# One transfer for the first weights of two pairs, sums inside the first pass, and no accumulating transfers, in a hybrid decoder step

## The chip, the cores and the metric

The kernel runs on one core of one Trainium2 chip. The metric is the device time of one execution in microseconds (us), lower is better. TensorE (PE) multiplies; VectorE (DVE), ScalarE (ACT) and GpSimd (POOL) work on elements; SyncE (SP) issues most transfers between the chip's memory and the core's on-chip memory.

## The reference: what is computed

One layer of a decoder for 256 new prompt tokens and 8 sequences of 4 new tokens each, 288 tokens in all, in float32. D_MODEL is 2048, the two head groups are 1024 wide each, the MLP is 8192 wide.

```python
def trunk_layer(x, hist_conv, hist_pool, pos0, ...):
    h = rmsnorm(x, norm1_g)
    proj = jnp.einsum("btd,de->bte", h, w_in) + b_in
    a, gate, z = proj[..., :D_CONV], proj[..., D_CONV:2 * D_CONV], proj[..., 2 * D_CONV:]
    u = a * jax.nn.sigmoid(gate)
    u_ext = jnp.concatenate([hist_conv, u], axis=1)
    c = jax.nn.silu(layernorm(depthwise_causal_conv(u_ext, conv_w, conv_b), ln_g, ln_b))
    z_ext = jnp.concatenate([hist_pool, z], axis=1)
    d = multiscale_pool(z_ext, pos0)          # window means (2, 4, 8, 16) minus z
    p = jnp.einsum("btgc,gce->btge", d, pool_w).reshape(bsz, T, D_POOL) * pool_scale
    x = x + jnp.einsum("btm,md->btd", jnp.concatenate([c, p], axis=-1), w_out)
    h2 = rmsnorm(x, norm2_g)
    f = jnp.square(jax.nn.relu(jnp.einsum("btd,df->btf", h2, w_ff1)))
    x = x + jnp.einsum("btf,fd->btd", f, w_ff2)
    return x, u_ext[:, -(CONV_W - 1):], z_ext[:, -(POOL_MAX - 1):]
```

A last RMSNorm follows, and the last 30 columns of u and 15 of z are returned too. The convolution has 31 taps.

## The kernel before, in words

Channels lie on the 128 partitions, the 288 tokens along the free side. Every product is made of float32 numbers split in two: `whi` is the weight rounded by a cast on ScalarE (L245), `wlo` the rest. A product of one 128x128 block takes three matmuls: `whi` by the high part of the activation (L284), `whi` by its low part (L285), `wlo` by the high part (L286). `gemm` runs over 16 blocks `k` of the contraction and two output halves `m`, 96 matmuls of 288 columns in all.

Weights arrive as tiles `wr` of 128x1024 (four k, both m) from a pool of six buffers, and their two parts lie in pools of five buffers each. `split_part` makes the low part in one of three ways, which the table `WAYS` picks by stage and turn: V subtracts on VectorE (L250), G on GpSimd in two halves (L253), D lets ScalarE write minus the high part into `wlo` (L247) and then has GpSimd issue a transfer that reads the weights once more from memory and adds them to it (L248). In the stage of the input projection D is taken once in each of the five blocks c3 to c7 and once in each of the four blocks p0 to p3.

The order of the work: a first pass makes the projections c0 and c1 ("both pairs") while x and the first weights land, k by k, in pieces (`first_pieces`, `first_split`). The norm's scale is not known by then; the pass multiplies x times the norm's gain, and `squares` sums the squares of x on ScalarE and VectorE. `rsqrt_sums` sums these over the channels with one-column matmuls on TensorE (`pt`, L211) and takes the inverse root; `spread` brings it to all partitions with a matmul (L230), and ScalarE copies it to `rb`. Then come the blocks of `SEQUENCE`: c2 to c7 (a convolution channel block each, with `conv_pair` behind it), p3 to p0 (the pooling groups) and P3 to P0 (their small products). `conv_pair` makes 31 products and sums on VectorE into `pc` and lastly into `c` (L398), with low priority, and GpSimd adds up `sum_c` (L407).

Then the output projection: its pooling half for the 8 column groups (`project_pool`, three groups before the layer norm of c and five in the middle of it), with the layer norm between: the mean on TensorE (`pmean`, L496), squares, `rsqrt_sums`, `spread`, then `n` on VectorE (L510), SiLU on ScalarE (L513), the high part by a cast (L515) and the low part on VectorE (L516) into `mx`, which the convolution half of the projection multiplies. The MLP runs in four chunks of 2048 columns.

Each engine runs its instructions strictly in the order in which they stand. A scheduler sets that order when the program is built, from priorities and its own timing of a simulated execution; the chip's timing has no part in it.

## Time and profile before

| | us |
|---|---|
| runs of the kernel | 1120.42, 1119.5, 1112.89 (median 1119.5) |
| the profiled execution | 1119.96 |
| its span, first to last instruction | 1118.2 |
| TensorE busy in the span | 1095.2 (98%) |
| VectorE, ScalarE, GpSimd busy | 628.6, 480.1, 178.4 |
| mean granted TensorE clock | 0.988 |

The profile names an instruction by its line in the kernel, its engine, its operation and its tiles (written tile, arrow, read tiles). Busy time of matmuls that overlap is counted once. "<-" behind an idle time names what the engine waited for. The granted clock is 1.00 at full speed. Times in windows are us from the start of the span.

### The profile page before, as it was taken

How to read it: one execution, taken by the hardware profiler on the slowest of the kernel's cores; microseconds unless marked ns; L12 is line 12 of the kernel's file. 1: busy time of each engine (PE TensorE's matmuls, PEld its weight loads, DVE VectorE, ACT ScalarE, POOL GpSimd, SP SyncE). 2: the span in 40 equal slices, each digit the busy share in tenths (PEclk: the TensorE clock that was granted, in tenths of full speed). 3: DMA queues.
4: the chain of work that ended last, by engine and by line, in shares of the span. 5: the costliest groups of instructions: out<-in, count | busy, mean ns of one | idle time of the engine just before them, and what ended most of it. 6: DMA issues, size and time to landing. Idle time of an engine off the chain costs nothing.

```text
span 1118.2 us, 19782 instructions
## 1 busy us (share of the span) xinstructions
PE 1095.2 (98%) x8214; PEld 1091.9 (98%) x8214; DVE 628.6 (56%) x825; ACT 480.1 (43%) x595; POOL 178.4 (16%) x217
## 2 busy tenths in 40 slices
PE   8999979999999999999999999999999999999995
PEld 8999979999999999999999999999999999999994
DVE  7599997668654544445554444544544445554453
ACT  8544544466444433334443333444433334444441
POOL 0689977903100000000000000000000000000000
PEclk9999999999999999999999999999999999999997
DMA  9886667545454455545555455554455544555522
GB/s 309 260 231 182 195 177 191 189 152 178 162 164 163 165 169 169 165 165 164 168 170 163 167 164 168 170 165 163 164 169 169 164 164 165 169 170 163 167 68 85
DMA packets 58553, 191.76 MB, mean 171 GB/s; under 512 B 6368, under 2 KB 11488, under 8 KB 58464
## 3 DMA queue, kind: packets, MB, share of 16 engines
q1 hardware_dynamic: 56880, 185.65, 50.6%
q0 software_dynamic: 1296, 4.72, 2.4%
q8 instruction: 64, 1.05, 0.4%
q14 instruction: 25, 0.20, 0.0%
q10 hardware_dynamic: 288, 0.14, 0.0%
HBM read 186.20 MB, written 4.28 MB: 170 GB/s over the span
## 4 chain that ended last, share of the span: by engine, by line
PE 93%; DMA 3%; POOL 1%; DVE 1%; ACT 0%; SPq 0%; issue 0%; DVEq 0%; POOLq 0%; ACTq 0%
PE ac L284 31%; PE ac L286 31%; PE ac L285 30%; DMA wlo<-in_w 3%; DMA wr<-in_w 1%; PE pt L211 1%; POOL wlo L253 1%; DVE xT L600 0%; POOL prd L402 0%; ACT whi L245 0%; PE pt L230 0%; POOL s L427 0%; PE pp L284 0%; SPq L176 0%; SPq L173 0%
## 5 line engine op out<-in xcount | busy, mean ns | idle before, releaser
L245 ACT CAST whi<-wr 128x1024 fp32r<-128x1024 f32 (+2 forms) x350 | 356.4, 1021 | 580.0 <-PE ac L285 558.4
L250 DVE TENSOR_TENSOR wlo<-wr,whi 128x1024 fp32r<-128x1024 f32 (+2 forms) x300 | 358.9, 1199 | 354.7 <-ACT whi L245 353.8
L284 PE MATMUL ac<-ax,whi 128*128 128x288 f32 x1024 | 303.2, 296 | 0.0
L284 PE MATMUL ac<-fx,whi 128*128 128x288 f32 x1024 | 303.1, 296 | 0.0
L286 PE MATMUL ac<-fx,wlo 128*128 128x288 f32 x1024 | 301.9, 295 | 0.0
L286 PE MATMUL ac<-ax,wlo 128*128 128x288 f32 x1024 | 301.8, 295 | 0.0
L285 PE MATMUL ac<-ax,whi 128*128 128x288 f32 x1024 | 299.8, 293 | 0.0
L285 PE MATMUL ac<-fx,whi 128*128 128x288 f32 x1024 | 298.5, 292 | 0.0
L285 PEld LDWEIGHTS ac<-ax,whi 128*128 128x128 f32 x1024 | 192.6, 188 | 0.1
L285 PEld LDWEIGHTS ac<-fx,whi 128*128 128x128 f32 x1024 | 192.5, 188 | 0.0
L284 PEld LDWEIGHTS ac<-ax,whi 128*128 128x128 f32 x1024 | 192.4, 188 | 0.1
L284 PEld LDWEIGHTS ac<-fx,whi 128*128 128x128 f32 x1024 | 192.4, 188 | 0.0
L286 PEld LDWEIGHTS ac<-ax,wlo 128*128 128x128 f32 x1024 | 192.3, 188 | 0.0
L286 PEld LDWEIGHTS ac<-fx,wlo 128*128 128x128 f32 x1024 | 191.5, 187 | 0.0
L286 PE MATMUL ac<-hx,wlo 128*128 128x288 f32 x384 | 114.0, 303 | 6.5 <-DMA wlo<-in_w 6.4
L284 PE MATMUL ac<-hx,whi 128*128 128x288 f32 x384 | 116.0, 303 | 2.4 <-ACT whi L245 2.2
L253 POOL TENSOR_TENSOR wlo<-wr,whi 128x512 fp32r<-128x512 f32 x82 | 107.4, 1367 | 51.8 <-ACT whi L245 51.7
L285 PE MATMUL ac<-hx,whi 128*128 128x288 f32 x384 | 114.5, 299 | 0.0
L398 DVE SCALAR_TENSOR_TENSOR pc<-u_all,vec,pc 128x256 f32<-128x256 f32 x232 | 99.2, 482 | 3.1 <-ACT pc L395 1.8
L286 PEld LDWEIGHTS ac<-hx,wlo 128*128 128x128 f32 x384 | 73.7, 194 | 7.5 <-DMA wlo<-in_w 7.4
L284 PEld LDWEIGHTS ac<-hx,whi 128*128 128x128 f32 x384 | 74.7, 195 | 3.1 <-ACT whi L245 3.1
L285 PEld LDWEIGHTS ac<-hx,whi 128*128 128x128 f32 x384 | 74.6, 194 | 0.1
(111 smaller groups left out, 822.9 us busy)
## 6 DMA issues: line engine op xcount, KB each, us to landing
wr<-in_w SPq DMA_DIRECT2D x328, 512.0 KB, 3.6
wr<-in_w SPq DMA_DIRECT2D x18, 256.0 KB, 5.6
wlo<-in_w POOLq DMA_DIRECT2D x9, 512.0 KB, 7.5
xT<-in_xT SPq DMA_DIRECT2D x7, 288.0 KB, 5.7
out_u_out<-u_all SPq DMA_DIRECT2D x1, 1208.0 KB, 8.4
out_yT<-xT SPq DMA_DIRECT2D x2, 576.0 KB, 3.1
u_all<-in_hist_c SPq DMA_DIRECT2D x8, 136.0 KB, 5.0
out_z_out<-z_all SPq DMA_DIRECT2D x1, 668.0 KB, 9.2
```

The lines of the kernel that those rows point to most:

```text
L211: nc.tensor.matmul(pt[:TB, j : j + 1], t[:, j * TB : (j + 1) * TB], ones[:, 0:1], start=n == 0, stop=n == len(parts) - 1)
L245: nc.scalar.copy(hi, raw)
L250: nc.vector.tensor_tensor(lo, raw, f32(hi), op=ALU.subtract)
L253: nc.gpsimd.tensor_tensor(lo[:, j : j + 2, :], raw[:, j : j + 2, :], f32(hi[:, j : j + 2, :]), op=ALU.subtract)
L284: nc.tensor.matmul(b, wh, xh, start=k == 0, stop=False)
L285: nc.tensor.matmul(b, wh, xl, start=False, stop=False)
L286: nc.tensor.matmul(b, wl, xh, start=False, stop=k == n - 1)
L398: nc.vector.scalar_tensor_tensor(out=dst, in0=up[:, w : w + SEQ], scalar=cwv[:, w : w + 1], in1=pc, op0=ALU.mult, op1=ALU.add)
```

## The change

Six edits are made together.

1. The first weights of a k come for both pairs in one transfer. A tile `wr` of the first pass now holds two k of both pairs instead of four k of one pair, and so do its `whi` and `wlo`; ScalarE and VectorE split both pairs in one instruction.
2. The first weight transfer is issued on ScalarE's queue ahead of the norm's gain; six pieces instead of seven are issued ahead of the set-up.
3. `squares` ends with two additions on VectorE, so that one part instead of four goes into the one-column matmuls, and it is called inside the first pass at k = 15. `rsqrt_sums` stands there too, and `spread` at k = 1 of c2 instead of k = 4. `tc.issue_after` holds the matmuls that follow behind these.
4. No stage uses D any more: c goes from GDGG to GGGV, p from GDVG to GVVG.
5. `ident` is padded by 40 elements, and `ax45` starts 32 elements into its buffer.
6. `rsqrt_sums` and `spread` also return their last matmul.

```diff
-WAYS = {"first": "VVVVVVVV", "c2": "GVGV", "c": "GDGG", "p": "GDVG", "w": "GG", "ff": "VV"}
+WAYS = {"c2": "GVGV", "c": "GGGV", "p": "GVVG", "w": "GG", "ff": "VV"}
...
-    def first_pieces(k, n):
-        if k % 4 == 0:
-            raws.append([raw_tile() for i in range(2)])
+    def by_pair(t):
+        return t[:].rearrange("p (i k) c -> p i k c", i=2)
+
+    def first_weights(k, n, queue):
+        if k % 2 == 0:
+            raws.append(by_pair(raw_tile()))
+        src = io["w"][1 + k // 8 : 4 + k // 8 : 2].rearrange("b p k c -> p b k c")
+        queue.dma_start(raws[-1][:, :, k % 2 : k % 2 + n, :], src[:, :, k % 8 : k % 8 + n, :])
+
+    def first_x(k, n):
         nc.sync.dma_start(xT[:, k : k + n, :], io["xT"][:, k : k + n, :])
-        for i in range(2):
-            queue = nc.scalar if k == 0 and i == 0 else nc.sync
-            queue.dma_start(raws[-1][i][:, k % 4 : k % 4 + n, :], io["w"][1 + 2 * i + k // 8][:, k % 8 : k % 8 + n, :])
 
     FIRST = [(0, 1), (1, 1)] + [(k, 2) for k in range(2, KT, 2)]
+    first_weights(0, 1, nc.scalar)
     nc.scalar.dma_start(vec[:, 0:NG], io["vec"][:, 0:NG])
-    for k, n in FIRST[:7]:
-        first_pieces(k, n)
+    for k, n in FIRST[:6]:
+        first_x(k, n)
+        if k > 0:
+            first_weights(k, n, nc.sync)
...
-    ident = const.tile([TB, TB], F32, name="ident")
+    ident = const.tile([TB, TB], F32, name="ident", padded_shape=[TB, TB + 40])
...
         for k, m in order:
-            if m == 0 and k in between:
-                between[k]()
+            if m == 0:
+                ahead = between[k]() if k in between else None
             (xh, xl), b = rhs[k], banks[m][:, :T]
             wh, wl = gets[k // 8](k % 8, m)
-            nc.tensor.matmul(b, wh, xh, start=k == 0, stop=False)
-            nc.tensor.matmul(b, wh, xl, start=False, stop=False)
-            nc.tensor.matmul(b, wl, xh, start=False, stop=k == n - 1)
+            with tc.issue_after(ahead.ins) if ahead is not None else nullcontext():
+                nc.tensor.matmul(b, wh, xh, start=k == 0, stop=False)
+                nc.tensor.matmul(b, wh, xl, start=False, stop=False)
+                last = nc.tensor.matmul(b, wl, xh, start=False, stop=k == n - 1)
...
-            split_part(raws[k0 // 4][i][:, at, :], None, hi[:, at, :], lo[:, at, :], WAYS["first"][k0 // 4 * 2 + i])
+        if k0 % 2 == 0:
+            firsts.append([by_pair(t) for t in spl()])
+        at = slice(k0 % 2, k0 % 2 + n)
+        raw, hi, lo = (t[:, :, at, :] for t in (raws[k0 // 2], *firsts[k0 // 2]))
+        split_part(raw, None, hi, lo, "V")
...
+        nc.vector.tensor_tensor(tot[0], tot[0], tot[1], op=ALU.add)
+        nc.vector.tensor_tensor(tot[0][:, 0, :], tot[0][:, 0, :], tot[0][:, 1, :], op=ALU.add)
+        return [tot[0][:, 0, :]]
...
-    gemm(pair0 + pair1, hx)
-    squares()
-    third = conv_products(
-        2,
-        between={
-            0: lambda: diag.append(rsqrt_sums([t[:, m, :] for t in tot for m in range(2)], 1.0 / D, AF.Sigmoid)),
-            4: lambda: nc.scalar.copy(rb, spread(diag[0])),
-        },
-    )
+
+    def first_sums():
+        diag.append(rsqrt_sums(squares(), 1.0 / D, AF.Sigmoid))
+        return diag[0][2]
+
+    def first_rows():
+        pr, last = spread(diag[0])
+        nc.scalar.copy(rb, pr)
+        return last
+
+    with tc.issue_after(gemm(pair0 + pair1, hx, between={15: first_sums})):
+        third = conv_products(2, between={1: first_rows})
...
-                ax45 = zp.tile([P, 2, 2, 2, T], F32R, name="ax45", tag="z", padded_shape=[P, 2, 2, 2, N8 * ZL // 8])
+                ax45 = zp.tile([P, N8 * ZL], F32R, name="ax45", tag="z")
+                ax45 = ax45[:, 32 : 32 + 8 * T].rearrange("p (g m q t) -> p g m q t", g=2, m=2, q=2)
```

The scheduler makes a new order of it, on all engines. Three places follow; the lines of the changed kernel stand 8 to 18 further on (L261 is the old L253, L258 the old L250, L411 the old L398, L239 the old L230).

GpSimd from c2 to c4, before: `wlo` are low parts (those of 128x512 by subtraction, two at a time), `prd` the products of the sample tokens' convolution.

```order
L253 TENSOR_TENSOR wlo_485<-wr_480,whi_484 128x512 x2
L468 MEMSET z_all 128x8x15
L253 TENSOR_TENSOR wlo_638<-wr_633,whi_637 128x512 x2
L248 DMA wlo_643<-in_w 128x1024
L253 TENSOR_TENSOR wlo_652<-wr_647,whi_651 128x512 x2
L402 TENSOR_TENSOR prd_701<-u_all,vec 128x8x31 x4
L402 TENSOR_TENSOR prd_745<-u_all,vec 128x8x31 x4
L253 TENSOR_TENSOR wlo_657<-wr_649,whi_656 128x512 x2
```

The same place in the changed kernel:

```order
L484 MEMSET z_all 128x8x15
L261 TENSOR_TENSOR wlo_491<-wr_486,whi_490 128x512 x2
L261 TENSOR_TENSOR wlo_604<-wr_599,whi_603 128x512 x2
L261 TENSOR_TENSOR wlo_609<-wr_601,whi_608 128x512 x2
L415 TENSOR_TENSOR prd_666<-u_all,vec 128x8x31 x4
L415 TENSOR_TENSOR prd_710<-u_all,vec 128x8x31 x4
L261 TENSOR_TENSOR wlo_618<-wr_613,whi_617 128x512 x2
```

The accumulating transfer of c3's second part (`wlo_643`) has become a subtraction here (`wlo_609`), and c3's fourth part (`wlo_657`) has left GpSimd.

VectorE in the convolution of channel blocks 0 and 1, before: `pc` are the products with the 31 taps, `ac` the results of c2, scaled by `rb`, and `c` the sums for the sample tokens.

```order
L398 SCALAR_TENSOR_TENSOR pc_669<-u_all,vec,pc_669 128x256 x3
L380 TENSOR_TENSOR ac_509<-ac_509,rb_268 128x288
L398 SCALAR_TENSOR_TENSOR pc_669<-u_all,vec,pc_669 128x256
L404 TENSOR_REDUCE c_668<-prd_701 128x32
L380 TENSOR_TENSOR ac_509<-ac_509,rb_268 128x288
```

The same in the changed kernel:

```order
L411 SCALAR_TENSOR_TENSOR pc_634<-u_all,vec,pc_634 128x256 x7
L417 TENSOR_REDUCE c_633<-prd_666 128x32
L411 SCALAR_TENSOR_TENSOR pc_634<-u_all,vec,pc_634 128x256
L258 TENSOR_TENSOR wlo_623<-wr_615,whi_622 128x1024
L411 SCALAR_TENSOR_TENSOR pc_634<-u_all,vec,pc_634 128x256
L393 TENSOR_TENSOR ac_500<-ac_500,rb_241 128x288
```

The fourth part of c3 (`wlo_623`) now stands among the products. The products begin earlier against c2's results.

TensorE at the spread of the layer norm's scale, before: `dx` are the pooling group's activations in `project_pool`, `mx` those behind the layer norm.

```order
L285 MATMUL ac_2788<-dx_2101,whi_2777 128x288
L286 MATMUL ac_2788<-dx_2101,wlo_2778 128x288
L230 MATMUL pt_2542<-dg_2563,ones 128x288
L284 MATMUL ac_2788<-dx_2101,whi_2777 128x288
L285 MATMUL ac_2788<-dx_2101,whi_2777 128x288
L286 MATMUL ac_2788<-dx_2101,wlo_2778 128x288
L284 MATMUL ac_2852<-dx_1292,whi_2846 128x288
```

The same in the changed kernel:

```order
L294 MATMUL ac_2809<-dx_2059,whi_2798 128x288
L295 MATMUL ac_2809<-dx_2059,wlo_2799 128x288
L239 MATMUL pt_2499<-dg_2520,ones 128x288
L293 MATMUL ac_2872<-mx_2529,whi_2862 128x288
L293 MATMUL ac_2943<-mx_2529,whi_2925 128x288
L294 MATMUL ac_2872<-mx_2529,whi_2862 128x288
L295 MATMUL ac_2872<-mx_2529,wlo_2863 128x288
```

Before, 51 matmuls of `project_pool` stand between the spread and the first matmul on `mx`; now the first matmul on `mx` is the next row. The second matmul of the mean (`pmean`) has moved from row 1443 of TensorE to row 1483, the one-column matmuls of the layer norm from row 1504 to row 1562, and the spread from row 1546 to row 1596.

28 lines of the change are left out of this document (12 added, 16 removed).

## The prediction

> **What bounds the kernel now.** I read the page first, then busy time in 10 us stretches, then the waits of TensorE, then its clock around each gap.
>
> ```profile
> span 1118.2 us, 19782 instructions
> PE 1095.2 (98%) x8214; PEld 1091.9 (98%) x8214; DVE 628.6 (56%) x825; ACT 480.1 (43%) x595; POOL 178.4 (16%) x217
> ```
>
> TensorE is busy for all but 23 us of the span. The change takes away only 18 one-column matmul records, so it can act only on gaps and on the clock. Busy time by stretch (columns: length, then PE, PEld, DVE, ACT, POOL with instruction counts, granted clock, DMA share, GB/s):
>
> ```profile
> 100.00:110.00 10.00, 10.00 (x78) 10.00 (x77) 10.00 (x26) 3.57 (x6) 9.49 (x9) 1.00 0.57 181
> 140.00:150.00 10.00, 7.88 (x57) 7.64 (x57) 10.00 (x21) 4.18 (x9) 7.52 (x11) 0.97 0.80 200
> 160.00:170.00 10.00, 6.41 (x41) 6.17 (x40) 10.00 (x17) 3.79 (x8) 7.69 (x10) 0.82 0.97 228
> ...
> PE ac L286 <- DMA wlo<-in_w: 6.4, 3, 3.6
> PE ac L284 <- ACT whi L245: 2.2, 1, 2.2
> ```
>
> A full stretch issues 78 matmuls; the two bad ones issue 57 and 41. All waits of TensorE up to 260 us are four: three for an accumulating transfer (6.4 us) and one at the start (2.2 us). Two of the three in the chain that ended last, from issue to landing:
>
> ```profile
> 140.00 8.00 DMA wlo<-in_w
> ...
> 158.45 9.22 DMA wlo<-in_w
> ```
>
> The clock adds to each gap (PE alone: length, busy, count, granted clock):
>
> ```profile
> 9.00:11.24 2.24, 0.00 (x0) 1.00 1.02 374
> 12.79:16.20 3.41, 3.41 (x17) 0.50 0.91 274
> 145.91:149.32 3.41, 1.29 (x10) 1.00 0.84 276
> 149.32:152.74 3.42, 3.42 (x17) 0.50 0.45 156
> 164.00:168.00 4.00, 0.41 (x2) 0.80 1.04 307
> 168.00:173.22 5.22, 5.22 (x23) 0.50 1.07 237
> ```
>
> A gap of about 2.1 to 2.2 us is followed by 3.4 us at half clock, which loses 1.7 us; the gap of 3.6 us by 5.2 us of work at half clock, which loses 2.6 us. The Trainium skill ("TensorE: Matmul & The Clock Gate", Part 1) puts the fall to half rate after an idle window of about 3.4 us; here 2.1 us was enough. By that rule the two short gaps would have cost 1.7 us less each, and so would a new short gap.
>
> **The change part by part.** *No accumulating transfers.* Gone: the 6.4 us of waits and their half clock, 1.7 + 2.6 us, together **-10.7 us**. The work goes elsewhere:
>
> ```profile
> L247 ACT ACTIVATE wlo<-whi 128x1024 fp32r<-128x1024 f32 x9 | 9.5, 1059 | 0.2
> ...
> L248 POOL DMA_DIRECT2D wlo<-in_w x9 | 8.2, 910 | 4.3 <-ACT prd L400 2.5 <-ACT wlo L247 1.3 <-POOL wlo L253 0.5
> ...
> L250 DVE TENSOR_TENSOR wlo<-wr,whi 128x1024 fp32r<-128x1024 f32 x6 | 11.7, 1948 | 3.2 <-ACT whi L245 3.2
> ...
> L250 DVE TENSOR_TENSOR wlo<-wr,whi 128x1024 fp32r<-128x1024 f32 x30 | 36.7, 1223 | 13.1 <-ACT whi L245 13.1
> ```
>
> The groups by form are of 26 to 208 us and of 208 to 320 us. ScalarE loses nine instructions of 1.06 us, GpSimd nine issues of 0.91 us. In the five blocks of kind c the subtraction moves from transfer to GpSimd and another from GpSimd to VectorE; in the four of kind p from transfer to VectorE. So VectorE gets nine subtractions, at 1.22 us where GpSimd is little used and 1.95 us in this stretch: 11.0 to 17.5 us. I take 17.5, the row from the same stretch. The Trainium skill ("SBUF — State Buffer", Who interferes with whom) says that a VectorE instruction with two SBUF inputs contends with a GpSimd instruction that reads SBUF; the two rows of one form agree, and it speaks against moving these subtractions to VectorE. Without contention the sum would take 11.0.
>
> Does it reach the end? VectorE's products of the convolution must end before the sum over channels, and TensorE's mean waits for that:
>
> ```profile
> 44.60:208.00 163.40, 147.09 (x311) 0.97 0.69 195
> ...
> DVE dx L451 <- ACT dx L450: 5.6, 3, 4.6
> ...
> 206.77 0.48 DVE L398 SCALAR_TENSOR_TENSOR c<-u_all,vec,pc 128x256 f32<-128x256 f32 x1
> ...
> 209.69 0.80 POOL L407 TENSOR_TENSOR sum_c<-sum_c,c 128x288 f32<-128x288 f32 x1
> ...
> 214.69 0.48 PE pmean L496 x2
> ```
>
> Before, VectorE worked 147.1 of 163.4 us here, ended at 207.2, and the mean came 4 us after the last sum (210.5): covered only because TensorE was late itself. That cover goes. TensorE would now be at the mean at 214.7 - 10.7 - 1.5 (sums, below) + 40 rows that now stand ahead of it. The step of a row:
>
> ```profile
> 340.35 0.76 DVE L565 SCALAR_TENSOR_TENSOR t<-ac,r 128x576 f32<-128x576 f32 x1 [0.99 <-PE ac L286]
> 353.07 0.76 DVE L565 SCALAR_TENSOR_TENSOR t<-ac,r 128x576 f32<-128x576 f32 x1 [0.99 <-PE ac L286]
> ```
>
> 96 matmuls take 12.72 us, 0.1325 each, so 40 are 5.3 us: 207.8. VectorE starts earlier, since the scales of the norm come earlier:
>
> ```profile
> 20.39 0.42 PE L211 MATMUL pt<-ones,z_all 128*96 128x1 f32 x4
> ...
> 35.79 1.78 PE L211 MATMUL pt<-ones,z_all 128*96 128x1 f32 x20
> ...
> 43.72 0.49 PE pt L230 x2
> ...
> 44.24 0.40 ACT L465 COPY rb<-pt 128x288 f32<-128x288 f32 x1 [1.31 <-PE pt L230]
> ```
>
> The sums now stand 12 matmuls before the end of the first pass (1.6 us before 35.8) and the spread 18 rows behind them, about 36.6 instead of 43.7; ScalarE has two casts of the size of L247 (1.06 us) ahead of the copy, so I take 6 us earlier (0 to 7). VectorE's end is then 207.2 - 6 + 17.5 + 0.8 (one more addition into the residual stands ahead, of the size of L358 below) - 4.6 (the wait for dx behind the gap at 164 us) = 214.9 if its other 11.7 us of idle time stay. An engine that runs behind finds more of its inputs ready; I take half of them gone: 209.0. With the short subtraction it is 202.5. Behind it come 0.8 us of sum on GpSimd, 209.8, so TensorE waits 2.0 us at the mean (bounds 0 and 8) and loses 1.7 us of clock: **+3.7 us**. GpSimd itself is relieved by 8.2 us of issues, so I cost its own waits at nothing; its cover is the slack of half a block that its subtractions have now, and if that is gone a wait is as long as one pair of subtractions, some 2.5 us.
>
> *Sums inside the first pass.* 24 records become 6. The two rows above begin the next work after 0.28 and 1.64 us, 1.9 us in all, so **-1.5 us**. VectorE gets an addition of about 0.76 and one of half its size (row below), hidden while the last blocks are multiplied. The spread moves to 18 rows (2.4 us) behind the sums. Its chain on VectorE and ScalarE, some ten instructions under 0.3 us, must fit into that; ScalarE no longer casts a late block ahead of it, so I take no wait, with 2 us as its bound.
>
> ```profile
> L358 DVE TENSOR_TENSOR z_all<-z_all 128x576 f32<-128x576 f32 x6 | 4.6, 760 | 0.1
> ...
> 10.57 1.26 ACT L245 CAST whi<-wr 128x512 fp32r<-128x512 f32 x2 [0.94 <-DMA wr<-in_w]
> ```
>
> *First weights in one transfer.* 18 transfers of weights become nine, but the bytes up to the third and fourth block are the same 1.6 MB (288 KB of x, two times 256 KB of weights, 288 of x, 512 of weights). TensorE's gap at 9 us ends when they land and ScalarE has cast them (10.57). Eight issues of SyncE up to them become five, but the cast now waits for 512 KB instead of 256. I take 0; bounds -3.9 (the gap and its half clock gone) and +1. On SyncE the last of these transfers now stands behind a vector and a history load and waits there for its buffer:
>
> ```profile
> 17.52 1.07 SPq L176 DMA_DIRECT2D wr<-in_w  x2
> ```
>
> Before it was issued by 18.6, and TensorE needs it 24 matmuls before the sums at 35.8, at 32.6: 14 us of cover, so nothing.
>
> *Aligned buffers.* The rows of the two halves of the MLP:
>
> ```profile
> L285 PE MATMUL ac<-ax,whi 128*128 128x288 f32 x1024 | 299.8, 293 | 0.0
> L285 PE MATMUL ac<-fx,whi 128*128 128x288 f32 x1024 | 298.5, 292 | 0.0
> ```
>
> The matmuls that read the moved buffer among others are 1.3 us slower in sum here. I take **-0.4 us**, bounds 0 and -1.3.
>
> *The other order at the layer norm.* In before 51 rows stand between the spread of the norm's scale and the first matmul on its result; in the change none. What the trace shows behind the spread, which started at 229.94:
>
> ```profile
> 230.46 1.42 DVE L510 TENSOR_TENSOR n<-c,pt 128x576 f32<-128x576 f32 x2 [1.04 <-PE pt L230]
> ...
> 231.68 2.19 ACT L513 ACTIVATE n<-n,vec 128x288 f32<-128x288 f32 x4
> 233.76 0.66 ACT L515 CAST mx<-n 128x576 fp32r<-128x576 f32 x1
> ...
> 234.45 0.76 DVE L516 TENSOR_TENSOR mx<-n,mx 128x576 fp32r<-128x576 f32 x1 [0.77 <-ACT mx L515]
> ...
> L284 PE MATMUL ac<-mx,whi x128: 293/294/298, 237.0 to 287.4; 128*128 128x288 f32 x128
> ```
>
> From the end of the spread (230.4) to the low part (235.2) are 4.8 us, hidden under project_pool before (first matmul on mx 237.0). Two matmuls can run earlier, and ScalarE's order now is the same two times two activations ahead of the cast: TensorE stands for 4.4 us and then loses 2.6 us as behind the 3.6 us gap: **+7.0 us** (bounds 3 and 8).
>
> **The sum:** -10.7 + 3.7 - 1.5 + 0 - 0.4 + 7.0 = -1.9 us. The profiled execution took 1119.96 us (span 1118.2 and 1.8 around it), so 1118.1; it stood 0.5 us above the median of 1119.5, so I say **1118 us**.
>
> **The rivals.** *The gains stand and the costs don't:* the start's gap closes (-3.9) and VectorE pays the short price, so no wait at the mean (-3.7): 1110. For it: half of ScalarE's cast instructions at the start are gone, and after 208 us the short subtraction is the rule. Against it: the same bytes, and GpSimd busy 9.5 of 10 us in the stretch.
>
> *VectorE becomes the bound (slower than before):* its other idle time stays, it ends at 214.9, the sum at 215.7, TensorE waits 7.9 instead of 2.0 us and loses 2.6 to 3.4 us of clock: +7.3 us over the forecast, **1125**. It decides from an end of VectorE at about 211, where the loss at mean and norm outweighs the 12.6 us won. For it: VectorE is busy 10.0 of 10 us in both bad stretches and gets more. Against it: the earlier start.
>
> *A wait in place of the removed one:* GpSimd's or VectorE's subtraction comes late at the blocks where the transfer did, three times 1 to 2 us, some with 1.7 us of clock: 1122 to 1126.
>
> **How the numbers follow.** Forecast 0.60, first rival 0.17, second 0.15, third 0.08. The range, 1109 to 1127, reaches from the first rival's end with the alignment's bound to the second's with another 2 us at the start or the spread. About 1% (11 us) is what a measurement of this kernel tells from no change; its own runs went from 1112.9 to 1120.4. Under 1108.3 lies half of the first rival and a little beside it, 0.12. Over 1130.7 lies a part of the second and third together, 0.09. Within 1%: 0.79.
>
> **What would show it.** Right: no row of TensorE waiting for a transfer of wlo; one wait of about 4 us at the matmuls on mx near 225 us, with half clock behind it; a short wait at the mean near 208 us; L411 ending near 209; subtractions of 128x1024 on VectorE near 1.9 us between 40 and 208 us; the copy to rb near 38. Wrong: no wait before mx, as then the order did not hold the norm's chain bare; a wait at the mean over 5 us, or none; a gap before the third block far from 2 us; new waits of L295 for wlo between 50 and 190 us.

## The result: 1106.6 us, 1% faster, below the forecast's range

| | before | changed |
|---|---|---|
| median of 15 runs each, us | 1118.56 | 1106.61 |
| lowest and highest, us | 1112.89, 1122.29 | 1104.71, 1113.68 |
| the profiled execution (its span), us | 1119.96 (1118.2) | 1111.87 (1110.1) |

The ratio is 0.991 (95% interval 0.9892 to 0.9929). The forecast was 1118 us, the range 1109 to 1127. The changed kernel's times lie in two groups, ten of them between 1104.7 and 1107.8 us and five between 1111.7 and 1113.7; the profiled execution belongs to the second. So there are two questions: what took 8.1 us off between the two profiles, and what are the further 6 us of the first group.

The head of the changed kernel's page:

```profile
span 1110.1 us, 19698 instructions
PE 1089.5 (98%) x8196; PEld 1086.4 (98%) x8196; DVE 640.2 (58%) x827; ACT 470.8 (42%) x577; POOL 181.5 (16%) x208
```

And its waits of TensorE (us in total, times, longest; left out are the set-up and the last norm's sums):

```profile
PE ac L293 <- ACT mx L531: 3.8, 1, 3.8
PE pt L239 <- DVE dg L233: 2.9, 2, 1.9
...
PE ac L293 <- ACT hx L317: 0.6, 1, 0.6
PE ac L295 <- POOL wlo L261: 0.6, 1, 0.6
PE pp L293 <- DVE dx L464: 0.5, 1, 0.5
PE ac L294 <- DVE mx L532: 0.3, 1, 0.3
```

No row waits for a transfer of wlo. New are the wait at mx, about 1 us at the first norm's spread (of the second row; the rest is the last norm's), and two of half a microsecond near 167 and 172 us. There is none at the mean (L512). Where the time went, from the start times of the same matmuls in both traces (us):

| stretch of TensorE | before | changed | difference |
|---|---|---|---|
| to the 289th matmul on hx (first pass, first norm, c2) | 50.66 | 48.44 | -2.2 |
| to the last on hx (c3 to c7, the pooling groups) | 130.33 | 118.32 | -12.0 |
| to the last on dx (pooling, mean, sums of the layer norm) | 55.88 | 56.84 | +1.0 |
| to the first on ax (layer norm, convolution's half) | 50.90 | 57.50 | +6.6 |
| MLP, first on ax to last on fx | 814.59 | 813.78 | -0.8 |
| the rest, to the start of the last instruction | 15.77 | 15.13 | -0.6 |

The matmuls in a row are the same, but for 18 one-column records in the first row and the two records of the layer norm's spread, 0.65 us, which pass from the third row to the fourth. The copy to rb stands at 36.84 us (44.24 before). VectorE's time line at the last products and the mean, changed kernel:

```profile
199.38 0.48 DVE L411 SCALAR_TENSOR_TENSOR c<-u_all,vec,pc 128x256 f32<-128x256 f32 x1
202.43 0.76 DVE L505 TENSOR_TENSOR xT<-xT,ac 128x576 f32<-128x576 f32 x1 [2.57 <-PE ac L295]
207.94 0.75 DVE L515 TENSOR_TENSOR c<-c,pmean 128x576 f32<-128x576 f32 x1 [4.76 <-PE pmean L512]
```

VectorE is done with the products at 199.86 and stands 4.8 us for the mean: it waits for TensorE, not the reverse. Its busy time from the first product to the last is the fourth number of a row (behind length, PE and PEld). Before:

```profile
49.20:207.25 158.05, 151.55 (x1109) 150.45 (x1108) 144.34 (x303) 76.73 (x105) 136.48 (x149) 0.97 0.68 194
```

Changed:

```profile
41.84:199.86 158.02, 156.96 (x1189) 156.40 (x1188) 153.83 (x313) 73.00 (x101) 147.42 (x146) 1.00 0.57 177
```

And the row of its subtractions by form, 36 to 208 us, changed kernel:

```profile
L258 DVE TENSOR_TENSOR wlo<-wr,whi 128x1024 fp32r<-128x1024 f32 x14 | 21.9, 1562 | 0.2 <-ACT whi L253 0.2
```

And the layer norm, where TensorE stands from the spread's end (224.4) to 228.2: the chain on VectorE, on ScalarE, and the half clock that follows (columns as in the prediction; 15 matmuls in 3.41 us), three views of the changed kernel:

```profile
224.60 1.41 DVE L526 TENSOR_TENSOR n<-c,pt 128x576 f32<-128x576 f32 x2
...
228.16 0.76 DVE L532 TENSOR_TENSOR mx<-n,mx 128x576 fp32r<-128x576 f32 x1 [1.01 <-ACT mx L531]
```

```profile
225.38 2.18 ACT L529 ACTIVATE n<-n,vec 128x288 f32<-128x288 f32 x4 [0.54 <-DVE n L526]
227.47 1.23 ACT L531 CAST mx<-n 128x576 fp32r<-128x576 f32 x2
```

```profile
229.11:232.52 3.41, 3.41 (x15) 3.41 (x16) 1.80 (x3) 2.18 (x5) 0.00 (x0) 0.50 0.26 95
```

### The profile page after: what moved, and what is told of

It is laid out like the page before. It is cut to its first block, busy times and chain, and to the rows that moved or that the text cites. A ratio compares the mean times of both kernels' runs of the same rounds, so it can differ in the third digit from the quotient of the medians.

```text
span 1110.1 us, 19698 instructions
## 1 busy us (share of the span) xinstructions
PE 1089.5 (98%) x8196; PEld 1086.4 (98%) x8196; DVE 640.2 (58%) x827; ACT 470.8 (42%) x577; POOL 181.5 (16%) x208
## 4 chain that ended last, share of the span: by engine, by line
PE 90%; DVE 6%; POOL 2%; issue 1%; ACT 0%; DMA 0%; DVEq 0%; ACTq 0%; POOLq 0%
PE ac L293 30%; PE ac L295 30%; PE ac L294 29%; DVE pc L411 3%; POOL s L440 1%; DVE wlo L258 1%; POOL wlo L261 1%; DVE xT L617 0%; PE pt L220 0%; DMA vec<-in_vec 0%; DVE dx L452 0%; POOL prd L415 0%; DVE dx L464 0%; DVE c L417 0%; PE pt L239 0%
## 5 line engine op out<-in xcount | busy, mean ns | idle before, releaser
L253 ACT CAST whi<-wr 128x1024 fp32r<-128x1024 f32 (+1 forms) x341 | 355.6, 1043 | 569.8 <-PE ac L294 530.5
L258 DVE TENSOR_TENSOR wlo<-wr,whi 128x1024 fp32r<-128x1024 f32 (+1 forms) x300 | 371.9, 1240 | 352.3 <-ACT whi L253 351.5
L261 POOL TENSOR_TENSOR wlo<-wr,whi 128x512 fp32r<-128x512 f32 x82 | 108.7, 1350 | 35.3 <-ACT whi L253 35.3
L293 PE MATMUL ac<-hx,whi 128*128 128x288 f32 x384 | 113.7, 299 | 0.6 <-ACT hx L317 0.6
L294 PE MATMUL ac<-hx,whi 128*128 128x288 f32 x384 | 112.8, 296 | 0.0
L295 PE MATMUL ac<-hx,wlo 128*128 128x288 f32 x384 | 110.8, 295 | 0.0
L411 DVE SCALAR_TENSOR_TENSOR pc<-u_all,vec,pc 128x256 f32<-128x256 f32 x232 | 98.6, 479 | 0.9
L293 PEld LDWEIGHTS ac<-hx,whi 128*128 128x128 f32 x384 | 72.8, 191 | 1.0 <-ACT hx L317 0.9
L294 PEld LDWEIGHTS ac<-hx,whi 128*128 128x128 f32 x384 | 72.9, 190 | 0.1
```

Of the source, the lines that this page charges most:

```text
L253: nc.scalar.copy(hi, raw)
L258: nc.vector.tensor_tensor(lo, raw, f32(hi), op=ALU.subtract)
L261: nc.gpsimd.tensor_tensor(lo[:, j : j + 2, :], raw[:, j : j + 2, :], f32(hi[:, j : j + 2, :]), op=ALU.subtract)
L293: nc.tensor.matmul(b, wh, xh, start=k == 0, stop=False)
L294: nc.tensor.matmul(b, wh, xl, start=False, stop=False)
L295: last = nc.tensor.matmul(b, wl, xh, start=False, stop=k == n - 1)
```

## The experiments

**1. The changed kernel again (e1), no edit.**

> The changed kernel once more, unchanged, as the level for the three runs beside it and to see whether the gaps repeat from one execution to the next. By the account of waits: 1106 to 1108 us, 9 to 13 us under the kernel before; TensorE waits about 4 us at the first matmuls on mx near 225 us, about 1 us at the spread of the first norm near 35 us, nothing at the mean, and the MLP takes 813.8 us from its first matmul on ax to its last on fx. The rival, that executions of one kernel stand at different levels without any wait: the same gaps, and yet a span that differs by 4 us or more from the 1110.1 us of the first profile, spread over the MLP's 814 us or beside the span.

1106.78 us (1105.14 to 1113.17, ratio 0.9916, 0.9888 to 0.9945). The profile shows the same waits to 0.2 us, the same clock, and a span of 1103.8 instead of 1110.1 us. The MLP alone took 807.07 instead of 813.77 us, evenly spread. The stretch of 400 to 1080 us of before, of the first and of this second profile of the changed kernel (first number in brackets: matmuls):

```profile
400.00:1080.00 680.00, 680.00 (x5140) 680.00 (x5139) 325.75 (x309) 264.26 (x286) 0.00 (x0) 1.00 0.50 165
```

```profile
400.00:1080.00 680.00, 680.00 (x5145) 680.00 (x5144) 325.51 (x308) 265.22 (x287) 0.00 (x0) 1.00 0.51 163
```

```profile
400.00:1080.00 680.00, 680.00 (x5188) 680.00 (x5188) 328.40 (x313) 266.68 (x291) 0.00 (x0) 1.00 0.51 163
```

At the same clock, with no wait, 43 more matmuls: a step of 0.1311 us instead of 0.1322. Over the 6,144 matmuls of the MLP that is 6.7 us, the distance of the two groups. The rival named here was right. I call the two the shorter and the longer step.

**2. Before without accumulating transfers (e2), 3. the changed kernel with them (e3).**

In the table `WAYS`, the rest of it unchanged:

```diff
e2 -"c": "GDGG", "p": "GDVG"   +"c": "GGGV", "p": "GVVG"     (in before.py)
e3 -"c": "GGGV", "p": "GVVG"   +"c": "GDGG", "p": "GDVG"     (in after.py)
```

> The kernel before with the table of ways alone changed (GDGG to GGGV, GDVG to GVVG); the norm's sums, the first weights and the alignment stay as before. In its order the second matmul of the mean stands at row 1506 of TensorE (1443 before), the layer norm's spread 15 rows behind its sums and nothing between it and mx. By the account of waits: the three waits for wlo go (-10.7 us with their half clock); VectorE, which starts at 49 us here, ends between 206.6 us (1.56 us a subtraction, its idle time filled) and 214 us (1.95 us); the mean comes at 212.3 us, so a wait of 0 to 3 us; at the layer norm a wait of about 2 us at the spread and 4 us at mx and 2.6 to 3.4 us of half clock, +9. Sum 1117 to 1122 us, no change against before. The rival, that the sums' place and the first weights bring nothing and removing the transfers brings the whole gain: 1106 to 1109 us.

> The changed kernel with only the table of ways put back (GDGG, GDVG), so that nine accumulating transfers stand in it again; sums, first weights and alignment as changed. In its order 51 rows stand between the layer norm's spread and mx, as in the kernel before. By the account of waits: three or so waits for wlo come back, 6.4 us and 4.3 us of half clock, and the wait at mx with its half clock (4.1 and 1.7 us) goes: +5, so 1111 to 1113 us. The rival, that the first pass and the alignment carry the gain and the transfers nothing: 1101 to 1104 us, since only the wait at mx goes.

e2: 1114.52 us (ratio 0.9977, 0.995 to 1.0003). No wait for wlo and none at the mean, although VectorE began its products at 47.1 us; it ended at 202.1. From 12 to 300 us TensorE waited once:

```profile
PE ac L284 <- ACT mx L515: 5.0, 1, 5.0
```

So the transfers go, and the bare layer norm comes with them: it is the new order of the table of ways alone that leaves nothing between spread and mx. The stretch of the first result table from c3 to the last matmul on hx took 118.87 us here, against 130.33 before. The time is 2.5 us under what was expected, and as a whole not clearly different from before; the expected wait at the spread did not come.

e3: 1118.0 us (1.0008, 0.9983 to 1.0034), 6 us above what was expected. Part of this is waits:

```profile
PE ac L295 <- DMA wlo<-in_w: 4.9, 4, 1.7
PE pp L294 <- DVE dx L452: 2.8, 1, 2.8
```

Its span is 6.3 us above the changed kernel's first profile, which has a wait and half clock of 5.8 at mx that e3 lacks: the transfers' order costs 12 us here, near the forecast's 10.7. Only 4.9 us of it are waits for transfers, though; 2.8 us are one wait for dx at 124.9 us, and 6.83 us of half clock begin there. The rest of the miss is the step: its profile runs the MLP at 0.1322, and its ten times (1117.2 to 1123.4) show no group 6.7 us lower.

**4. Work between spread and mx (e4).**

```diff
-    rl = rsqrt_rows([x[:, m, :] for x in (ssc, q) for m in range(2)], 1.0 / DC, AF.Silu)
+    sums_ln = rsqrt_sums([x[:, m, :] for x in (ssc, q) for m in range(2)], 1.0 / DC, AF.Silu)
+    rl, spread_ln = spread(sums_ln)
...
-    project_pool(range(3, 8))
+    project_pool(range(3, 8), between={7: {0: lambda: sums_ln[2], 3: lambda: spread_ln}})
```

> The changed kernel with the order at the layer norm alone held: the one-column sums stand ahead of the last group of project_pool (row 1542 of TensorE instead of 1562), the spread 18 rows behind them, and 30 rows of that group stand between the spread and the first matmul on mx. By the account of waits: the sums are ready at 215.3 us and stand at 215.6; a wait of about 1 us at the spread (its chain takes 4 us from the sums, the rows 3) and 0.8 us at mx instead of 4.1, and no half clock behind either: -4 us, 1102 to 1104 us. The rival, that the chain on VectorE and ScalarE is late anyway (they cast and subtract weights in between) or that the clock falls behind a short wait as well: within 1 us of the changed kernel.

1108.91 us (1107.59 to 1110.57; 0.9931, 0.9907 to 0.9956), 5 us above what was expected. The waits at mx went as expected; the first two rows are TensorE's from 12 to 300 us, the others busy time around the layer norm's sums (columns as in the prediction):

```profile
PE ac L293 <- ACT mx L532: 0.5, 1, 0.5
...
PE ac L294 <- DVE mx L533: 0.3, 1, 0.3
...
214.80:218.20 3.40, 3.40 (x36) 3.27 (x34) 2.62 (x7) 1.81 (x3) 0.00 (x0) 1.00 0.65 224
218.20:221.60 3.40, 3.40 (x15) 3.12 (x14) 0.80 (x5) 0.93 (x2) 0.00 (x0) 0.51 0.49 171
```

Span 1107.1, 2.9 us under the first profile of the changed kernel, not 4: half clock follows the one-column sums, which are dense in records and light in work. That is a property of the execution and not of this order: e12 and e18 have the same order here and no half clock, and a third profile of the changed kernel (e13) has it, from 220.7 us. Within a profile the stretches of half clock begin whole multiples of 3.41 us apart (before: 12.79, 149.32 and 166.39 us). Laid out at these distances, the intervals hold the sums' 2.0 us whole, to 0.07 us, in the nine profiles with half clock behind the sums; in the ten without it the sums cross from one interval into the next (in e2 with their last record alone). e7, which waits at the sums, is left out. And yet the median is 2 us above the changed kernel's, since none of the ten times lies in the lower group: the MLP of its profile runs at 0.1322.

**5. The sums back behind the first pass (e5).**

```diff
-    with tc.issue_after(gemm(pair0 + pair1, hx, between={15: first_sums})):
-        third = conv_products(2, between={1: first_rows})
+    gemm(pair0 + pair1, hx)
+    third = conv_products(2, between={0: first_sums, 4: first_rows})
```

> The changed kernel with the first norm's sums and spread put back behind the first pass (sums in c2's first block, spread in its fifth, nothing holding the matmuls behind them); the two additions on VectorE stay. In its order the sums stand at TensorE's row 194 (182 in the changed kernel), the spread at 219 (201), the mean at 1483 in both. What it tells: whether the earlier start of VectorE is what keeps TensorE from waiting at the mean. If VectorE's idle time simply closes: rb near 41 us instead of 37, the products end near 202 us all the same, no wait at the mean, and the time is within 2 us of the changed kernel. If the start decides, as in the forecast's sum: the products end 4 us later than now, 204 us or more, and with the sum over channels behind it TensorE waits 0 to 2 us at the mean; in the worst case +4 us.

1106.57 us (four runs, 1104.66 to 1111.27; 0.9901, 0.987 to 0.9931), no difference. The matmuls behind sums and spread stay held, other than the expectation says. The profiled execution was the longest, though it ran the MLP at the shorter step: there the spread waited 3.7 us for dg, TensorE came 4.7 us later to the mean (211.9), and VectorE ended at 205.6, its sum over channels at 208.4. Set against the changed kernel's 207.3 at the mean, an undisturbed TensorE would have waited about 1 us, by estimate. The earlier start is worth about that much at the mean.

**6. Without the alignment (e6).**

```diff
-    ident = const.tile([TB, TB], F32, name="ident", padded_shape=[TB, TB + 40])
+    ident = const.tile([TB, TB], F32, name="ident")
-                ax45 = ax45[:, 32 : 32 + 8 * T].rearrange(...)
+                ax45 = zp.tile([P, 2, 2, 2, T], F32R, name="ax45", tag="z", padded_shape=...)
```

> The changed kernel without the padding of ident and without the offset of ax45. By the account of rows: the MLP's halves that read ax take 0.1325 us a matmul instead of 0.1322 and the whole stage 0.8 us more, nothing else: 1107 to 1108 us. The rival, that alignment also decides how often the MLP runs at the shorter step (0.1311 us a matmul, seen in one profile of the changed kernel and not in the other): most executions then lie 6 us higher, 1112 to 1115 us.

1113.23 us, ten runs from 1112.24 to 1115.05 (0.9966, 0.9949 to 0.9983): the rival. It takes out both edits at once; which of the two matters was not tried. In the profile the step is 0.1311 us for 6.6 us behind the second norm's sums (293.8 us), and from the spread on 0.1322 on fx and 0.1325 on ax.

**7. Ten more subtractions on VectorE (e7).**

```diff
-WAYS = {"c2": "GVGV", "c": "GGGV", ...
+WAYS = {"c2": "GVGV", "c": "GVVV", ...
```

> The changed kernel with ten more subtractions of the blocks of kind c moved from GpSimd to VectorE (GGGV to GVVV). It prices one subtraction on VectorE where GpSimd has less to do, and finds where VectorE becomes the bound. If it costs 1.2 us each: +12 us of work, of which the 4 us of idle time take some, so the products end near 208 us; at 1.5 us each near 211, at 1.95 us each, the forecast's price, near 215. In its order the mean stands at TensorE's row 1565 (1483 in the changed kernel), reached near 218 us, with the norm's sums 25 rows behind it and the spread right behind these: so no wait at the mean, but about 5 us at the sums, 2 to 4 at the spread and 4 to 5 at mx, with half clock: 1115 to 1122 us, 8 to 15 over the changed kernel. The rival, that VectorE has room: within 2 us of the changed kernel.

1112.69 us (0.9958, 0.994 to 0.9975), 6 above the changed kernel and 2 under what was expected. The price by form (36 to 213 us), VectorE's busy time over its products, and the waits of TensorE over the whole span (1.9 us of the first row belong to the last norm):

```profile
L258 DVE TENSOR_TENSOR wlo<-wr,whi 128x1024 fp32r<-128x1024 f32 x26 | 35.4, 1360 | 2.7 <-ACT whi L253 2.6
...
41.85:212.45 170.60, 170.60 (x1295) 170.49 (x1294) 166.20 (x327) 76.84 (x105) 135.09 (x133) 1.00 0.58 179
...
PE pt L239 <- DVE dg L233: 4.8, 3, 1.9
PE pt L220 <- DVE q L521: 4.0, 1, 4.0
PE ac L293 <- ACT mx L531: 3.6, 1, 3.6
```

The mean price is 1.36 us; the busy time of the whole stretch grew by 12.4 us over the changed kernel's (166.20 less 153.83), 1.24 for each of the ten. The products end at 212.45, later than expected for 1.5 us each (211), since the 4 us of idle time stay (170.60 less 166.20). The mean, late by the order (215.9), waits for nothing. What VectorE's load costs appears at the sums and the spread of the layer norm, where the order has left no other work. (This profile runs at the shorter step, so its span of 1109.0 stands for 1115.7 beside the first profile's 1110.1.)

**8 to 11. What sets the step.** e8 and e10 add one-column matmuls into an unused bank at seven places of the MLP, e9 one such to e4, e11 those of e8 to e6.

```diff
+    def mark():
+        marks.append(1)
+        w = ms("mark")
+        for j in range(len(marks)):
+            m1 = nc.tensor.matmul(w[:, 0, j : j + 1], ones, ones[:, 0:1], start=True, stop=True)
+        return m1
...
-            gemm(each(bk), x1)
+            gemm(each(bk), x1, between={8: mark} if ch and g == 1 else {})
...
-            gemm(banks, fx, m_outer=last and g == 7)
+            gemm(banks, fx, between={8: mark} if g == 2 else {}, m_outer=last and g == 7)
```

> The changed kernel with seven interruptions added to the MLP: one-column matmuls into a scratch bank that nothing reads, one at the first place, two at the second, up to seven at the last, between the eighth and ninth block of a group. It asks whether the step of a matmul in the MLP (0.1322 us in one profile of the changed kernel, 0.1311 in the other, from about 293 us to the end) is set anew where TensorE is interrupted. If it is: the step differs between the eight stretches, and changes just at these places. If the step belongs to the execution: one step in all eight stretches. If it belongs to the reading of ax or fx: it goes by stage. The time is 2.4 us of added matmuls and some 1.5 us of their surroundings above the changed kernel where the steps are alike.

> The kernel of the filled layer norm (the order at the layer norm held) with a single one-column matmul into a scratch bank that nothing reads, in the third group of the MLP's first chunk, near 311 us. The filled kernel ran its whole MLP at 0.1322 us a matmul in its profile, and its ten times (1107.6 to 1110.6 us) show no execution 6.7 us shorter. If an odd number of one-column matmuls sets the shorter step of 0.1311 us, whatever the stage (so it was in the run with marks: one, three, five and seven were followed by it, two, four and six by the longer one): the MLP runs at 0.1311 us from the mark on, and the time is 1101.5 to 1103.5 us. If the stage decides (there the marks in the halves that read fx were followed by the shorter step, those in the halves that read ax by the longer): no change, 1107.6 to 1110.6 us.

> The run with marks again, at the same seven places, with two, one, four, three, six, five and eight one-column matmuls: the odd numbers now stand in the halves of the MLP that read ax, the even ones in those that read fx. If the number decides: the shorter step after the second, fourth and sixth mark (near 503, 706 and 910 us), the longer one after the others, the reverse of the first run. If the stage decides: as in the first run. If each interruption draws anew by chance: neither.

> The kernel without the padding and the offset, with the marks of the first run (one to seven). It asks why that kernel's ten times show none with the shorter step. If a block that reads the unaligned buffer ends the shorter step for good: after the marks with an odd number, which stand in the halves that read fx, the rest of that half runs at 0.1311 us, and from the first unaligned block of ax on the step is 0.1322 to 0.1328 us until the next odd mark. If the alignment has nothing to do with it: the same stretches as with the alignment, apart from the unaligned blocks themselves.

The step (ns, mean over the stretch; starts in us) in the three runs with seven marks, from the start times of the matmuls:

```
sums of norm 2 -> mark1(fx) -> mark2(ax) -> mark3(fx) -> mark4(ax) -> mark5(fx) -> mark6(ax) -> mark7(fx)
e8   from 293.5: 131.1  414.6: 131.1  503.0: 132.2  617.7: 131.1  706.4: 132.2  821.6: 131.1  910.8: 132.2  1026.4: 131.1
e10  from 295.6: 131.1  416.7: 131.1  505.3: 132.2  619.7: 131.1  708.7: 132.2  823.6: 131.1  913.1: 132.2  1028.4: 131.1
e11  131.1 to the spread at 301.4, then 132.2 to 132.5 everywhere
```

So the step can be set anew where TensorE is interrupted, here the same in both runs whatever the number of one-column matmuls; and without the alignment it neither stays short nor becomes short again behind a mark. e8 took 1114.74 us, e10 1116.12 and e11 1119.44 (one run each of these two). e9 changed nothing (1108.43 us, 132.2 on both sides of its mark): the place in a half that reads ax or fx was not yet the reason.

**12 to 14. Another mark (e12), the changed kernel beside it (e13), the alignment alone (e14).** e12 is e4 with one one-column matmul in the first half that reads fx; e14 is before.py with the two edits that e6 takes out.

> The kernel of the filled layer norm with a single one-column matmul into a scratch bank that nothing reads, now in the third group of the first half that reads fx, near 412 us. In both runs with marks all eight marks in such halves were followed by the shorter step, whatever the number of one-column matmuls, and the five behind which the step was looked for in halves that read ax by the longer. If the place decides: 0.1322 us a matmul until 412 us and 0.1311 from there to the end, some 5,100 matmuls by 0.0011 us, -5.6 us: 1103 to 1104 us. If the filled kernel cannot run at the shorter step: 1107.6 to 1110.6 us as without the mark.

> The changed kernel unchanged, beside the run before it on the same chip, so that the two can be compared: 1105 to 1108 us, with some executions near 1112 us that run the MLP at the longer step.

> The kernel before with the two edits of alignment alone (ident padded by 40 elements, ax45 moved by 32). By the forecast's term: -0.4 us, at most -1.3. By what the runs with marks show: the MLP can now run at the shorter step, from the sums of the second norm (near 300 us) on; the executions that do are 6.7 us shorter than those that don't, and all save 0.8 us: between -0.8 us (no execution has it) and -7.5 us (all have it) against the kernel before.

e12: 1108.99 us, its profile at 132.2 ns throughout the MLP; the place is not the reason. e13: 1105.69 us, five runs of 1105.0 to 1105.7 and four of 1112.1 to 1114.3. e14: 1117.44 us (1.0009, 0.9993 to 1.0024): the alignment alone brings nothing that the twelve runs show; its profile is at the longer step, and none of its times (from 1114.63 us) stands clearly under the rest. e14 shows something else. It waits for the transfers as before does:

```profile
PE ac L286 <- DMA wlo<-in_w: 7.0, 3, 3.1
```

Two of these gaps are of 2.9 and 3.1 us, and no half clock follows either: each lies across a boundary of the 3.41 us intervals, 1.2 to 1.8 us on a side. The 2.1 us gap of before, which half clock followed, lay within one. So c3 to the last matmul on hx took 127.0 us in e14, and 130.33 before.

**15 and 16. Is it the wait at the layer norm?** All kernels with the shorter step so far had that wait. e15 is e2 with the alignment; e16 is e4 with

```diff
+        for _ in range(6 if j == 0 else 0):
+            nc.scalar.copy(n, n)
         mh, ml = act2("mx")
```

> The kernel before with the table of ways and the two edits of alignment; sums and first weights as before. Theory: the MLP comes to the shorter step of 0.1311 us only where the buffers are aligned and TensorE has stood for some 4 us, with half clock behind it, ahead of it at the layer norm. So far all kernels with both had executions at about 1105 us (the changed kernel 20 of 33), and the 47 executions with the alignment but without that wait (the accumulating transfers put back, the filled layer norm, the alignment alone) had none. This kernel has both, as its order at the layer norm is bare: a wait of 5 us at mx. So more than a third of its executions fall 6 us or more under the rest, to 1105 to 1108 us, and the rest lies at 1112 to 1114. If the sums inside the first pass or the first weights are needed for it: all at 1111 to 1115 us.

> The kernel of the filled layer norm with six copies of the first activation onto itself on ScalarE (0.62 us each) between SiLU and the cast, which add nothing to the values and make TensorE wait at mx again, by about 4 us with half clock behind it. Filled and without them the ten times were 1107.6 to 1110.6 us, all at the longer step. If a wait of that size at this place is what lets the MLP come to the shorter step: some executions at the longer step, 1113 to 1115 us (5.5 us over the filled kernel), and more than a third 6.7 us under these, 1106 to 1108 us. If it is another property of the filled order: all at 1113 to 1115 us.

e15: 1113.78 us (1112.38 to 1116.05), e16: 1115.06 (1112.97 to 1117.55), the wait at mx 4.6 and 5.6 us, and no sign of the shorter step: both profiles are at 132.2 ns, and the times lie within 5 us. That theory fell.

**17 and 18. The phase of the sums.** The intervals between the start times of the last 13 matmuls ahead of the second norm's sums and from the last of them to the sums, in ns, with the step that follows, show a cycle of two block products (six matmuls) with one long matmul:

```
before      ... 132 133 132 133 137 126 132 | 133 133 132 | 138 126 130  -> 131.1 (until the spread)
changed     ... 132 138 125 132 133 133 132 | 138 126 131 | 134 132 133  -> 132.2
e1          ... 132 134 133 132 137 126 132 | 133 132 133 | 138 126 129  -> 131.1
e4          ... 133 137 126 132 133 133 132 | 138 125 132 | 133 133 132  -> 132.2
```

In 18 profiles the long matmul lay nine times in the last block product, and the shorter step followed; nine times in the last but one (changed, e3, e4, e9, e12 to e16), and the longer went on. So e17 holds sums and spread of e4 one block product later, e18 two. In both, the work of VectorE and ScalarE on the first two groups of the MLP moves behind the spread (its lines are left out here).

```diff
-            gemm(each(bk), x1)
-            if ch == 0 and g == 0:
-                nc.scalar.copy(r2, rsqrt_rows([ss2, q2], 1.0 / D))
+            gemm(each(bk), x1, behind={(0, 1): second_sums, (7, 1): second_spread} if ch == 0 and g == 1 else {})
...
(e18:                          behind={(1, 0): second_sums, (8, 0): second_spread})
```

> The kernel of the filled layer norm with the one-column sums of the second norm and its spread held one block product (three matmuls) later on TensorE: three, not no, matmuls of the MLP's second group stand ahead of the sums, and again 42 between sums and spread. Theory: the longer step is a cycle of six matmuls (two block products) of which one takes 0.137 to 0.138 us; in the 18 profiles so far the MLP goes on at the shorter step (until the spread at least) in the nine where the long matmul lies in the last block product ahead of the sums, and at the longer one in the nine where it lies in the last but one. The filled kernel is of the second kind in all its profiles. So here the long matmul lies in the last block product, the MLP runs at 0.1311 us a matmul from about 291 us on, and the time is 6.7 us under the filled kernel: 1101.5 to 1103.5 us. If the phase is not what decides: 1107.6 to 1110.6 us.

> The same with sums and spread two block products (six matmuls, one whole cycle) later. By the theory of the phase the long matmul lies in the last but one block product again and nothing changes: 0.1322 us a matmul, 1107.6 to 1110.6 us. If any move of the sums into the group brings the shorter step: 1101.5 to 1103.5 us.

e17: **1102.99 us** (four runs, 1101.42 to 1104.4; 0.9864, 0.9842 to 0.9886). e18: 1109.11 (1108.77 to 1109.91; 0.992, 0.9898 to 0.9943). The same stretch of the MLP, e17 and e18:

```profile
400.00:1080.00 680.00, 680.00 (x5189) 680.00 (x5187) 327.54 (x313) 266.25 (x290) 0.00 (x0) 1.00 0.51 162
```

```profile
400.00:1080.00 680.00, 680.00 (x5145) 680.00 (x5145) 326.06 (x310) 264.45 (x286) 0.00 (x0) 1.00 0.51 162
```

```
e17         ... 131 134 132 133 137 126 132 | 133 132 133 | 137 126 130  -> 131.1
e18         ... 133 137 126 132 133 132 133 | 137 126 132 | 133 133 132  -> 132.2
```

Between e17 and e18 the place of the sums and the spread differs by three matmuls, and the time by 6 us. e17 is under both kernels; its interval against before lies below the changed kernel's.

## Why the prediction was wrong, by its own steps

**Two terms failed.** The first is the alignment's. The prediction read the two MLP rows, saw 1.3 us between them, and wrote "-0.4 us, bounds 0 and -1.3". The stage itself moved within these bounds where the step stayed (-0.8 in the pair of profiles, both at the longer step). But without the alignment the MLP does not stay at the shorter step (e6: its profile, and no time in ten under 1112.2 us, +6.5 us in the median against e1; e11). With it, going by their times, 21 of the changed kernel's 33 runs have it (under 1108 us; ten lie over 1111, and two between cannot be told). In this kernel, then, alignment is needed, and it is not enough: the profiles of e3, e4, e14 and e15 are aligned and at the longer step. Two rows of one execution at one step could not show the other step; the traces of before held only a hint, 6.6 us at 131.1 ns between the second norm's sums and its spread.

The second is the wait at the mean, +3.7. TensorE was there when forecast (207.3 against 207.8), VectorE 9.1 us sooner (199.9 against 209.0). Of its three parts the start was 7.4 us earlier where I took 6, and the idle time closed by 9.5 us (158.05 less 144.34, to 158.02 less 153.83) where I took 4.6 and half of 11.7, 10.4. What failed is "I take 17.5, the row from the same stretch": VectorE's work grew by 9.5 us, not by 17.5 and 0.8. The old row of 1.95 us had six members; from 36 to 208 us, the stretch of the changed kernel's row above, it was, before:

```profile
L250 DVE TENSOR_TENSOR wlo<-wr,whi 128x1024 fp32r<-128x1024 f32 x5 | 9.6, 1914 | 1.8 <-ACT whi L245 1.8
```

With 14 members the mean is 1.56, so nine more cost 21.9 less 9.6, 12.3 us or 1.37 each, e7 gives 1.36, and other rows got shorter (the subtraction into dx from 1.58 to 1.24 us). The Trainium skill ("SBUF — State Buffer", Who interferes with whom) lets a VectorE instruction with two SBUF inputs contend with a GpSimd one that reads SBUF. The trace agrees, as 1.22 us is the rule where GpSimd does little, but the price here is 0.15 to 0.35 us, not 0.7.

**What held.** The transfers: -10.7 forecast, -12.0 in their stretch, -11.5 by e2, 12 by e3. The 4.3 us of half clock in that term were a draw of one execution, as e14 shows: against its 127.0 us the changed kernel's 118.32 are only 8.7 less. That a gap of 2.1 us is enough for half clock, as the prediction read it, holds for where that gap lay, and not for its length alone. The layer norm: +7.0 forecast, +6.6 in its row, 0.65 of which is the spread that now counts there; the waits of 3.8 and 0.3 us and the half clock, 1.7 us instead of 2.6, are where they were said to be, and e4 takes all but 0.8 us of the waits away. The Trainium skill ("TensorE: Matmul & The Clock Gate", Part 1) asks for an idle window of about 3.4 us; the trace differs once more, as e4 has half clock behind 3.4 us of 36 records without a gap.

**The small ones.** First weights, 0: right. The 97th matmul on hx starts at 20.4 to 23.1 us in four profiles of the old code and 20.3 to 22.5 in 16 of the new; the profile of before was the latest of the four, and most of the -2.2 of the first stretch is that draw. Sums, -1.5: the records went, but the spread now waits about 1 us for its chain (the bound said 2), and nothing is left: the 289th matmul starts at 47.9 to 48.6 us in the three other profiles of the old code, 47.8 to 48.9 in 13 of 15 of the new (e5, with the sums elsewhere, left out). I had bounded that wait and then not taken it. The waits near 167 and 172 us, +1.0, I had priced at nothing.

Summed over the pair of profiles: -2.2 - 12.0 + 1.0 + 6.6 - 0.8 - 0.6 = -8.0, against a forecast of -1.9. The median fell by 4 us more, since most of the changed kernel's runs are, by their times, at the shorter step. Without that the forecast's range would have held the result, as it holds the profiled execution.

**The rivals.** The first (1110 us) came nearest to the profiled execution, in part by luck: there was no wait at the mean, as it said, but the price was between short and long, and what the start gained is the draw above. It has no reason for the rest. The second, VectorE as the bound, did not come; e7 shows that even 22 us more of work than before (166.20 against 144.34) do not reach the mean, because the order moves the mean with them, and the cost comes out at the norm behind it. Of the third, a wait in place of the removed one, two of half a microsecond came, without half clock.

**Open.** Why a cycle of six matmuls has two forms, why alignment lets the shorter one stay, and what in the changed kernel makes the phase at the sums differ between its runs. Shown is only that the step behind the sums goes with their place within the cycle in all 20 profiles, and that a move of sums and spread by three matmuls changed it (e17 against e18). What was measured of the alignment is both edits together.

## What to carry to other kernels

A long stretch of equal matmuls can run at two steps that differ by under 1%; look at the count of matmuls per fixed window in several executions before a difference of a per cent is put down to waits. Price added instructions by how the busy time of the whole stretch grows, not by the longest row of a few members. A forecast of the time needs the new order's bare places (here the layer norm), since they move with any edit that changes a scheduler's view of the load. And the half clock behind a gap has to be looked at in more than one execution before it is counted as a cost of the gap.

## What the hardware showed that was not expected

A step of 131.1 or 132.2 ns for the same matmul, at full granted clock and without a wait, held for 800 us and set where TensorE is interrupted: 6.7 us of 1105. Without the two edits to the buffers' starts the shorter one ended at the spread (e6, e11). Half clock came behind one-column matmuls without a gap (e4, 3.41 us), and did not come behind gaps of 2.9 and 3.1 us (e14): where work and gaps lay in intervals of 3.41 us went with it. And a VectorE subtraction of 128x1024 took from 1.22 to 1.95 us on average by stretch and kernel, with the lower end where GpSimd had little to do.
